# Delta-rule values and two gated branch outputs turned by VectorE in blocks of 32 and through DRAM, in place of TensorE transposes

## The chip, the cores and the metric

The kernel runs on one core of one Trainium2 chip, as one launch. The metric is the device time in microseconds (us). The kernel before takes 1671.04 us (median of 3 runs, 1670.95 to 1672.13).

A core has engines that each work through their own list of instructions in order: TensorE (PE in the profile; its weight loads are PEld), VectorE (DVE), ScalarE (ACT), GpSimd (POOL) and SyncE (SP). They wait for each other by semaphores. SP and POOL issue the DMA transfers here: SP streams the weights in, POOL issues everything small.

## The reference

One decoder layer over 256 positions of width 2048, all in float32: `x + mixer(rms_norm(x))`, then `x + ffn(rms_norm(x))`, then a last norm. Three branches of the mixer are projected out of one matrix product, and the change concerns two of them, the delta rule (GDN, 8 value heads of 128) and the gated linear attention (GLA, 4 heads of 256):

```
h = rms_norm(x);  c_q, ..., gla_q, gla_k, gla_v, ..., gdn_qkv, ..., gdn_z, merge = split(h @ w_in)
# GDN: conv + SiLU gives q, k, v; per chunk of 64 a triangular solve with v
u0  = triangular_solve(t_mat, beta * v)
o   = rms_norm(delta_rule(...)) ;  y_gdn = o * silu(z)
# GLA: chunked scan with a decay for each key channel
o   = rms_norm(gla_scan(...))   ;  y_gla = o * silu(r)
mixed = sum_i sigmoid(merge_i) * (y_i @ w_branch_i);  x + mixed @ w_out
```

## The kernel before, in words

**Weights.** Every weight goes the same way, in pieces of 512 KB: SP loads `raw`; ACT writes its rounded part `hi` (`split_piece`, act.copy, L191 in the profile); DVE writes the rest, `lo` = raw - hi (the subtraction stands under L103, the line of the helper `tt`); PE multiplies with both. The stream pool holds four buffers each of `raw`, `hi` and `lo`, so ACT and DVE can be some four pieces ahead of PE and no more. `t_chunk` (L237 to L239) computes 256 positions by 512 columns into two banks of PSUM; `fj_chunk` (L212, L213) computes 256 columns by 256 positions, also into two banks (here with half-pieces' products side by side, added up afterwards).

**PSUM.** There are two groups of four banks: `acc` for these weight products, `mix` (tiles `ps`) for all else. A fifth `acc` tile takes the bank of the first, as soon as that has been read. A chunk of `fj_chunk` is read by `halves_sum` (L217 to L221): for both of its banks ACT copies one half out, and DVE adds the other half.

**Delta rule (GDN).** Its convolution leaves the values `gv` with channels on the partitions. Before the solves, PE transposes them (L781, 16 transposes of 128x128 into four `ps` tiles), and DVE scales them from PSUM into `vt` (four instructions 128x512). Solves and state updates follow for heads in pairs `gp`; each pair leaves `og` tiles (`o_gdn`, DVE copies at L834), of which ACT takes squares (`junk`, L840). Once all four `og` are there, DVE computes their inverse norms (a chain of small instructions, `m`, `rsy`, `rsa`, `fg`), and `gated_out` multiplies each `og` by its gate `zs` and by `fg`, has PE transpose it (L865, 16 in all), and splits the result from PSUM into `hi_y` (ACT, L293) and `lo_y` (DVE, L106), the operand of the branch's projection.

**GLA.** Then the memory of the region `r2` (which held the delta rule's tiles, among them four rotating buffers of the tag `t`) is given up and `r3` opened, in the same memory. GLA's query and key products `lq` and `lk` are computed by `fj_chunk` (two chunks each), its values `lv` and its gate (`gates_of(GLA_R)`) by `t_chunk`. Head by head, DVE and ACT then compute exponentials (tiles `E`) for small matmuls on PE; behind each head's work stands a quarter of the merge of the delta rule's branch, whose projection reads `hi_y` and `lo_y`. At the end `gated_out` runs for GLA's outputs `ol` (16 more transposes), into `hi_E` and `lo_E`.

**The order of the work.** The program is written in the order of the formulas; a scheduler of the tile framework then moves instructions within each engine's list, by its own model of their durations. A pool's tile that is reused waits for all who read the earlier one, DMA transfers out of it among them.

**A turn.** `turned` exists before, and is used for the merged outputs and the residual stream: DVE transposes each 32x32 block of a tile within its place (a STREAM_TRANSPOSE, L304), POOL issues a DMA that writes the tile to DRAM (L306), and four DMAs read it back with the blocks exchanged (L312).

Of the kernel before, what the change touches and what calls it, by code (L numbers as in the profile page):

```python
# [16 lines left out]
P = 128  # L17
# [38 lines left out]
def trunk(ctx, tc, A, out, dbg=None, stop=None):  # L56
# [4 lines left out]
    def nm(s):  # L61
        serial[0] += 1
        return f"{s}{serial[0]}"
# [18 lines left out]
    def S(tag, shape=(P, 512), dt=F32, n=None):  # L82
        p, bufs = pools[tag]
        return p.tile(list(shape), dt, name=nm(n or tag), tag=tag, bufs=bufs)

    def PS(n="ps"):
        return pp.tile([P, 512], F32, name=nm(n), tag="mix")
# [7 lines left out]
    def keep(shape, n, dt=F32):  # L95
        return cp.tile(list(shape), dt, name=n)
# [5 lines left out]
    def tt(o, a, b, op, eng=None):  # L102
        (eng or dve).tensor_tensor(o, a, b, op=op)  # L103
# [138 lines left out]
    def TH():  # L242
        return wp.tile([P, 512], F32, name=nm("th"), tag="th", bufs=4)
# [51 lines left out]

    def turned(src, tags, n=512):

        nk = n // P  # L300
        d = dp.tile([2 * P, n], F32, name=nm("d_t"))
        for t in range(2):
            v = S(tags[0], (P, n), n="tr")
            dve.transpose(v.rearrange("p (b k i) -> p k b i", b=4, k=nk),  # L304
                          src[t].rearrange("p (k b i) -> p k b i", b=4, k=nk))
            pool.dma_start(d[t * P:(t + 1) * P], v)  # L306
        dv = d.rearrange("(a j) (b k i) -> b j a k i", j=32, b=4, k=nk)
        res = []
        for g in range(nk // 2):
            r = S(tags[1], (P, 8, 2, 32), n="rd")  # L310
            for b in range(4):
                pool.dma_start(r[b * 32:(b + 1) * 32], dv[b, :, :, 2 * g:2 * g + 2])  # L312
            res.append(r)
        return res

# [320 lines left out]


    sel = keep([P, 68], "sel", F32R)
    pool.memset(sel.bitcast(F32), 0.0)
# [134 lines left out]
    for gp in ((0, 1), (2, 3)):  # L774

        vts = {}
        for g in gp:
            psb = PS().rearrange("p (t x) -> p t x", t=2)
            for a in range(2):
                for t in range(2):  # L780
                    pe.transpose(psb[:, t, a * P:(a + 1) * P], gvv[2 * g + a][:, t * P:(t + 1) * P], ident)  # L781
            vts[g] = S("vt", (P, 2, 2, P))
            tt(vts[g].rearrange("p t a d -> p t (a d)"), psb, vs[:, :, g:g + 1].to_broadcast([P, 2, 256]), MUL)
        for s in (32, 64):
# [70 lines left out]

    def gated_out(o_tiles, f_of, zs, gcol, name, ytag):

        y = Act(8, ytag)
        for g in range(4):
            o = o_tiles[g]  # L860
            f_of(g, o, [zs[t][g // 2][:, (g % 2) * 256:(g % 2) * 256 + 256] for t in range(2)])
            psb = PS()
            for a in range(2):
                for t in range(2):
                    pe.transpose(psb[:, a * 256 + t * P:a * 256 + (t + 1) * P], o[:, t, a, :], ident)  # L865
            gained(psb, [half_gain[:, gcol + 2 * g + a:gcol + 2 * g + a + 1] for a in range(2)], y)
            if dbg is not None and ("y_" + name) in dbg:
                full = S("t", (P, 2, 256), n="dbg")
                tt(full, y.hi[g].bitcast(F32), y.lo[g], ADD)
                sync.dma_start(dbg["y_" + name][:, 2 * g:2 * g + 2, :], full)  # L870
        return y
# [53 lines left out]

    y_gdn = gated_out(o_gdn, scale_gdn, zs, 8, "gdn", "y")
    if stop == "gdn":
# [18 lines left out]

    sr = gates_of(GLA_R, "rs", "d")


# [119 lines left out]

    y_gla = gated_out(o_gla, scale_gla, sr, 0, "gla", "E")  # L1070
    if stop == "gla":
# [208 lines left out]
```

## Time and profile before

| | |
|---|---|
| time, median of 3 runs | 1671.04 us |
| profiled execution | 1671.5 us, its span 1669.7 us, granted clock 0.998 |
| PE busy | 1656.2 us, 99% of the span |
| DVE busy | 1106.4 us, 66% |
| ACT busy | 828.0 us, 50% |
| POOL busy | 135.7 us, 8% |
| chain that ended last | PE 94%, DVE 1% |
| moved by DMA | 314.96 MB, 188 GB/s to and from HBM over the span |

The span is what the profile covers; 1.8 us of the execution's own time lie around it. "Busy" leaves waits out, and matmuls overlap each other, so a busy PE need not be PE at its peak. Times within the span are counted from its start.

### The profile page before, as it was taken

How to read it: one execution, taken by the hardware profiler on the slowest of the kernel's cores; microseconds unless marked ns; L12 is line 12 of the kernel's file. 1: busy time of each engine (PE TensorE's matmuls, PEld its weight loads, DVE VectorE, ACT ScalarE, POOL GpSimd, SP SyncE). 2: the span in 40 equal slices, each digit the busy share in tenths (PEclk: the TensorE clock that was granted, in tenths of full speed). 3: DMA queues.
4: the chain of work that ended last, by engine and by line, in shares of the span. 5: the costliest groups of instructions: out<-in, count | busy, mean ns of one | idle time of the engine just before them, and what ended most of it. 6: DMA issues, size and time to landing. Idle time of an engine off the chain costs nothing.

```text
span 1669.7 us, 23887 instructions
## 1 busy us (share of the span) xinstructions
PE 1656.2 (99%) x9068; PEld 1406.8 (84%) x9068; DVE 1106.4 (66%) x1740; ACT 828.0 (50%) x1157; POOL 135.7 (8%) x202
## 2 busy tenths in 40 slices
PE   9999999999999999999999999999999999999997
PEld 7898888888888888888888888888888888888886
DVE  6868798755755795755656766664566665556666
ACT  6555563433444654444445654454355553345454
POOL 1000032200000000002112000000000000000000
PEclk9999999999999999999999999999999999999999
DMA  7565556654565456568777665656666566665653
GB/s 267 147 201 153 158 155 190 206 155 148 160 186 192 153 189 180 174 204 254 231 225 244 205 190 190 188 188 190 194 193 191 189 190 191 193 191 187 199 186 117
DMA packets 181059, 314.96 MB, mean 189 GB/s; under 512 B 17786, under 2 KB 45106, under 8 KB 180944
## 3 DMA queue, kind: packets, MB, share of 16 engines
q1 hardware_dynamic: 175488, 301.83, 57.7%
q0 software_dynamic: 5424, 11.60, 2.4%
q8 instruction: 71, 1.16, 0.3%
q14 instruction: 44, 0.36, 0.1%
q10 hardware_dynamic: 32, 0.01, 0.0%
HBM read 307.63 MB, written 5.77 MB: 188 GB/s over the span
## 4 chain that ended last, share of the span: by engine, by line
PE 94%; DVE 1%; issue 0%; ACT 0%; ACTq 0%
PE acc L239 17%; PE acc L237 17%; PE acc L238 17%; PE acc L212 15%; PE mix L212 10%; PE acc L213 8%; PE mix L213 5%; PE acc L1204 0%; PE acc L1206 0%; PE acc L1205 0%; PE ps L542 0%; PE ps L543 0%; DVE lo L103 0%; DVE u L103 0%; PE ps L1026 0%; PE ps L796 0%
## 5 line engine op out<-in xcount | busy, mean ns | idle before, releaser
L103 DVE TENSOR_TENSOR lo<-raw,hi 128x1024 fp32r<-128x1024 f32 (+2 forms) x571 | 686.6, 1205 | 498.9 <-ACT hi L191 496.1
L191 ACT CAST hi<-raw 128x1024 fp32r<-128x1024 f32 (+2 forms) x555 | 582.1, 1049 | 702.4 <-PE acc L239 412.2
L212 PE MATMUL acc<-hl_h,hi 128*128 128x512 f32 x1088 | 383.5, 397 | 0.0
L213 PE MATMUL acc<-hl_h,lo 128*128 128x256 f32 x1088 | 304.5, 280 | 0.0
L238 PE MATMUL acc<-lo,hl_h 128*128 128x512 f32 x640 | 249.3, 392 | 0.0
L239 PE MATMUL acc<-hi,hl_h 128*128 128x512 f32 x640 | 248.8, 392 | 0.0
L237 PE MATMUL acc<-hi,hl_h 128*128 128x512 f32 x640 | 247.4, 392 | 0.1
L212 PE MATMUL mix<-hl_h,hi 128*128 128x512 f32 x704 | 246.3, 395 | 0.0
L212 PEld LDWEIGHTS acc<-hl_h,hi 128*128 128x128 f32 x1088 | 203.9, 188 | 47.1
L213 PEld LDWEIGHTS acc<-hl_h,lo 128*128 128x128 f32 x1088 | 205.0, 188 | 1.0
L213 PE MATMUL mix<-hl_h,lo 128*128 128x256 f32 x704 | 196.0, 278 | 0.0
L212 PEld LDWEIGHTS mix<-hl_h,hi 128*128 128x128 f32 x704 | 132.1, 188 | 31.6
L237 PEld LDWEIGHTS acc<-hi,hl_h 128*128 128x128 f32 x640 | 120.3, 188 | 25.6 <-ACT hl_h L293 0.5
L238 PEld LDWEIGHTS acc<-lo,hl_h 128*128 128x128 f32 x640 | 120.5, 188 | 24.7
L239 PEld LDWEIGHTS acc<-hi,hl_h 128*128 128x128 f32 x640 | 120.3, 188 | 24.7
L213 PEld LDWEIGHTS mix<-hl_h,lo 128*128 128x128 f32 x704 | 132.5, 188 | 0.0
L238 PE MATMUL acc<-lo,hi_f 128*128 128x512 f32 x320 | 124.3, 389 | 0.0
L237 PE MATMUL acc<-hi,hi_f 128*128 128x512 f32 x320 | 124.2, 389 | 0.0
L239 PE MATMUL acc<-hi,lo_f 128*128 128x512 f32 x320 | 124.0, 389 | 0.0
L103 POOL TENSOR_TENSOR fcv<-fcv,rbc 128x512 f32<-128x512 f32 x22 | 31.3, 1424 | 669.0 <-ACT fcv L1161 669.0
L239 PEld LDWEIGHTS acc<-hi,lo_f 128*128 128x128 f32 x320 | 60.1, 188 | 12.5
L237 PEld LDWEIGHTS acc<-hi,hi_f 128*128 128x128 f32 x320 | 60.1, 188 | 12.5
(407 smaller groups left out, 1928.8 us busy)
## 6 DMA issues: line engine op xcount, KB each, us to landing
raw<-in_w_in_dram SPq DMA_DIRECT2D x207, 512.0 KB, 3.4
raw<-in_ffn_w_up_dram SPq DMA_DIRECT2D x176, 512.0 KB, 3.7
raw<-in_ffn_w_down_dram SPq DMA_DIRECT2D x88, 512.0 KB, 4.6
raw<-in_w_out_dram SPq DMA_DIRECT2D x32, 512.0 KB, 4.7
raw<-in_w_branch_mla_dram SPq DMA_DIRECT2D x16, 512.0 KB, 3.8
raw<-in_w_branch_gdn_dram SPq DMA_DIRECT2D x16, 512.0 KB, 3.8
raw<-in_w_branch_gla_dram SPq DMA_DIRECT2D x16, 512.0 KB, 6.1
raw<-in_mla_w_ukv_dram SPq DMA_DIRECT2D x8, 512.0 KB, 4.5
```

What stands on the lines that cost most here:

```text
L103: (eng or dve).tensor_tensor(o, a, b, op=op)
L191: act.copy(hi[:, ks], raw[:, ks])
L212: pe.matmul(banks[f], hi[:, kt, fs], joint[k], start=k == 0, stop=False, skip_group_check=True)
L213: pe.matmul(banks[f][:, :T], lo[:, kt, fs], joint[k][:, :T], start=False, stop=k == nk - 1, skip_group_check=True)
L237: pe.matmul(o, ah, hi[:, kt, :], start=first, stop=False)
L238: pe.matmul(o, ah, lo[:, kt, :], start=False, stop=False)
L239: pe.matmul(o, al, hi[:, kt, :], start=False, stop=last)
```

## The change

Three transposes by PE are replaced.

- The delta rule's values: right after the decay `gdec`, DVE turns the blocks of each `gv` tile (4 STREAM_TRANSPOSE of 128x512 into tiles of the tag `t`), and POOL writes them to DRAM (`d_v`, 4 DMAs). Before each pair's solves, POOL reads them back with blocks exchanged (16 DMAs, `rd`), and DVE scales them into `vt` (8 instructions 128x256 instead of 4 of 128x512).
- The delta rule's outputs: `gated_out` now scales each `og` as before, and turns it out: 8 STREAM_TRANSPOSE of 128x256 into tiles `tr` of the tag `t`, which has four buffers, and 8 DMAs to DRAM. `gated_in` reads it back (16 DMAs, into tiles `th` of the stream pool) and splits it from SBUF into `hi_y` and `lo_y`. It is called a stage later, behind `gates_of(GLA_R)`.
- GLA's outputs: the same two functions, one right after the other, with tiles of the tag `lqkv`.

No transposes of PE remain in these three places: 48 fewer. ACT and DVE have the same number of splits. DVE has 20 block transposes more, POOL 68 more DMAs to issue.

```diff
-    def turned(src, tags, n=512):
+    def turn_out(src, tag, n=512):
         nk = n // P
         d = dp.tile([2 * P, n], F32, name=nm("d_t"))
         for t in range(2):
-            v = S(tags[0], (P, n), n="tr")
+            v = S(tag, (P, n), n="tr")
             dve.transpose(v.rearrange("p (b k i) -> p k b i", b=4, k=nk),
                           src[t].rearrange("p (k b i) -> p k b i", b=4, k=nk))
             pool.dma_start(d[t * P:(t + 1) * P], v)
...
+        return d.rearrange("(a j) (b k i) -> b j a k i", j=32, b=4, k=nk)
+
+    def turn_in(dv, g, tag):
+        r = S(tag, (P, 8, 2, 32), n="rd") if tag else TH().rearrange("p (a k i) -> p a k i", k=2, i=32)
+        for b in range(4):
+            pool.dma_start(r[b * 32:(b + 1) * 32], dv[b, :, :, 2 * g:2 * g + 2])
+        return r
...
+    d_v = []
+    for g in range(4):
+        v = S("t", (P, 4, 4, 32), n="tr")
+        dve.transpose(v.rearrange("p b k i -> p k b i"), gv[g].rearrange("p a (t b i) -> p (a t) b i", t=2, b=4))
+        d = dp.tile([P, 4, 4, 32], F32, name=nm("d_v"))
+        pool.dma_start(d, v)
+        d_v.append(d.rearrange("(a j) b k i -> b j a k i", j=32))
...
         for g in gp:
-            psb = PS().rearrange("p (t x) -> p t x", t=2)
-            for a in range(2):
-                for t in range(2):
-                    pe.transpose(psb[:, t, a * P:(a + 1) * P], gvv[2 * g + a][:, t * P:(t + 1) * P], ident)
+            r = S("t", (P, 4, 2, 2, 32), n="rd")
+            for b in range(4):
+                pool.dma_start(r[b * 32:(b + 1) * 32].rearrange("p c a t i -> p c (a t) i"), d_v[g][b])
             vts[g] = S("vt", (P, 2, 2, P))
-            tt(vts[g].rearrange("p t a d -> p t (a d)"), psb, vs[:, :, g:g + 1].to_broadcast([P, 2, 256]), MUL)
+            for t in range(2):
+                dve.tensor_scalar(vts[g][:, t].rearrange("p a (c i) -> p a c i", i=32),
+                                  r[:, :, :, t].rearrange("p c a i -> p a c i"), vs[:, t, g:g + 1], None, op0=MUL)
...
-    def gated_out(o_tiles, f_of, zs, gcol, name, ytag):
-        y = Act(8, ytag)
+    def gated_out(o_tiles, f_of, zs, tag):
+        res = []
         for g in range(4):
             o = o_tiles[g]
             f_of(g, o, [zs[t][g // 2][:, (g % 2) * 256:(g % 2) * 256 + 256] for t in range(2)])
-            psb = PS()
-            for a in range(2):
-                for t in range(2):
-                    pe.transpose(psb[:, a * 256 + t * P:a * 256 + (t + 1) * P], o[:, t, a, :], ident)
-            gained(psb, [half_gain[:, gcol + 2 * g + a:gcol + 2 * g + a + 1] for a in range(2)], y)
...
+            res.append(turn_out([o[:, t].rearrange("p a d -> p (a d)") for t in range(2)], tag, 256))
+        return res
+
+    def gated_in(dvs, gcol, ytag, tag):
+        y = Act(8, ytag)
+        for g in range(4):
+            gained_sb(turn_in(dvs[g], 0, tag),
+                      [half_gain[:, gcol + 2 * g + a:gcol + 2 * g + a + 1] for a in range(2)], y)
         return y
...
-    y_gdn = gated_out(o_gdn, scale_gdn, zs, 8, "gdn", "y")
+    d_gdn = gated_out(o_gdn, scale_gdn, zs, "t")
...
     sr = gates_of(GLA_R, "rs", "d")
+    y_gdn = gated_in(d_gdn, 8, "y", None)
...
-    y_gla = gated_out(o_gla, scale_gla, sr, 0, "gla", "E")
+    y_gla = gated_in(gated_out(o_gla, scale_gla, sr, "lqkv"), 0, "E", "lqkv")
```

Where the scheduler puts these instructions is seen in each engine's list. The number behind a tile's name tells one buffer from another, and differs between the two programs; "waits" names the semaphores for which a row waits: those of an engine, or those of POOL's DMAs (DMASW0 to 7, handed out in turn) and SP's (DMAHW).

**DVE, from the last `og` tiles to GLA's first query sums.** `og` are the delta rule's outputs, `zs` the gates, `m` the first tile of the inverse norms, `lq` GLA's queries, `acc` banks of PSUM. Before, this stood there:

```order
L834 COPY og_3096<-ps_3089 128x512 [waits PE_49]
L834 COPY og_3113<-ps_3106 128x512 [waits PE_49]
L103 TENSOR_TENSOR og_3096<-og_3096,zs_4367 128x256 [waits DVE_49,Activation_49]
L103 TENSOR_TENSOR og_3096<-og_3096,zs_4371 128x256 [waits Activation_49]
L103 TENSOR_TENSOR og_3113<-og_3113,zs_4367 128x256 [waits DVE_49,Activation_49]
L103 TENSOR_TENSOR lo_4603<-raw_4600,hi_4602 128x1024 [waits DMAHW0_49,PE_49,Activation_49]
L103 TENSOR_TENSOR m_3127<-m_3127,gst 128x16 [waits Activation_49]
L103 TENSOR_TENSOR og_3113<-og_3113,zs_4371 128x256
L951 COPY glr_5433<-few 16x256
L103 TENSOR_TENSOR lq_4433<-lq_4433,acc_4437 128x256 [waits Activation_49]
L103 TENSOR_TENSOR lq_4433<-lq_4433,acc_4438 128x256 [waits Activation_49]
```

Now the first query sum stands behind the whole scaling and the eight block transposes (the rows shown begin at the last product with `fg`):

```order
L103 TENSOR_TENSOR og_3133<-og_3133,fg 128x512
L302 STREAM_TRANSPOSE tr_4397<-og_2948 128x2x4x32 [waits DVE_49]
L302 STREAM_TRANSPOSE tr_4400<-og_2948 128x2x4x32
L302 STREAM_TRANSPOSE tr_4407<-og_2965 128x2x4x32 [waits DVE_49]
L302 STREAM_TRANSPOSE tr_4410<-og_2965 128x2x4x32
L302 STREAM_TRANSPOSE tr_4417<-og_3116 128x2x4x32 [waits DMASW5_49,DVE_49]
L302 STREAM_TRANSPOSE tr_4420<-og_3116 128x2x4x32 [waits DMASW6_49,DVE_49]
L302 STREAM_TRANSPOSE tr_4427<-og_3133 128x2x4x32 [waits DMASW7_49,DVE_49]
L302 STREAM_TRANSPOSE tr_4430<-og_3133 128x2x4x32 [waits DMASW0_49,DVE_49]
L964 COPY glr_5481<-few 16x256
L103 TENSOR_TENSOR lq_4437<-lq_4437,acc_4441 128x256 [waits DMASW4_49,Activation_49]
L103 TENSOR_TENSOR lq_4437<-lq_4437,acc_4442 128x256 [waits Activation_49]
```

The four block transposes that name a DMASW wait for the write of the tile that had their buffer (DMASW5, 6, 7 and 0 are the first four of the eight writes, in order), and the first sum for the eighth write (DMASW4): the memory of `lq` in `r3` was that of `r2`'s last `tr`. Between the two copies of `og` and this sum stands one weight piece's `lo`; none stands between that `lo` and the sum. ACT's copy of the same bank, on which the sum waits as well, waits for the same write.

**PE, the first product for GLA's keys** (`acc_4627` before, `acc_4631` now, the fifth `acc` bank from the first of the query chunks on). Before, the last rows ahead of it are the second query chunk's:

```order
L213 MATMUL acc_4533<-hl_h_209,lo_4603 128x256
L212 MATMUL acc_4533<-hl_h_219,hi_4602 128x512
L213 MATMUL acc_4533<-hl_h_219,lo_4603 128x256
L212 MATMUL acc_4533<-hl_h_220,hi_4602 128x512
L213 MATMUL acc_4533<-hl_h_220,lo_4603 128x256
L212 MATMUL acc_4627<-hl_h_142,hi_4631 128x512 [waits DVE_49,Activation_49]
```

Now they are the delta rule's last outputs (`ps_3126`, which the second copy to `og` reads):

```order
L213 MATMUL acc_4537<-hl_h_220,lo_4607 128x256
L844 MATMUL ps_3126<-W_3107,hq_2661 128x128 [waits DVE_49]
L842 MATMUL ps_3126<-W_3089,hq_2660 128x128
L843 MATMUL ps_3126<-W_3089,hq_2660 128x128
L844 MATMUL ps_3126<-W_3107,hq_2661 128x128
L212 MATMUL acc_4631<-hl_h_142,hi_4635 128x512 [waits DVE_49]
```

The solves and outputs of the delta rule stand later among the weight pieces than before. The DVE instruction for which the last row waits is the first query sum shown above (`lq_4437` with `acc_4441`).

**PE, where the merge of the delta rule's branch begins**, among GLA's first head (`hl_h` are the layer's inputs, for the merge gate; `hi_y` the branch's). Before, the merge gate's seventh piece is begun like this:

```order
L237 MATMUL acc_5605<-hi_5717,hl_h_208 128x512 [waits Activation_49]
L237 MATMUL acc_5606<-hi_5717,hl_h_208 128x512
L238 MATMUL acc_5605<-lo_5718,hl_h_208 128x512 [waits DVE_49]
L239 MATMUL acc_5605<-hi_5717,hl_h_208 128x512
L237 MATMUL acc_5605<-hi_5717,hl_h_209 128x512
```

Now two products of the branch's own first piece are in between:

```order
L237 MATMUL acc_5653<-hi_5765,hl_h_208 128x512 [waits Activation_49]
L237 MATMUL acc_5654<-hi_5765,hl_h_208 128x512
L237 MATMUL acc_5803<-hi_5807,hi_y_5442 128x512 [waits Activation_49]
L237 MATMUL acc_5804<-hi_5807,hi_y_5442 128x512
L238 MATMUL acc_5653<-lo_5766,hl_h_208 128x512 [waits DVE_49]
```

The new third row waits for ACT's cast of the branch's first piece (`hi_5807`), two pieces further on; in ACT's list that cast stands behind three pairs of `hi_y` splits, which before stood ahead of GLA's key sums, and behind exponentials of the first head.

More of the change, by code (lines that the diff above doesn't have):

```diff
@@ L306, in turned @@
             pool.dma_start(d[t * P:(t + 1) * P], v)
[L307 to L314, printed above, removed]
+        return d.rearrange("(a j) (b k i) -> b j a k i", j=32, b=4, k=nk)
[4 more added lines that the diff above has]
+        return r
+    def turned(src, tags, n=512):
+        dv = turn_out(src, tags[0], n)
+        return [turn_in(dv, g, tags[1]) for g in range(n // 256)]
     def gained_sb(r, gains, store):
@@ L861, in gated_out @@
             f_of(g, o, [zs[t][g // 2][:, (g % 2) * 256:(g % 2) * 256 + 256] for t in range(2)])
-            psb = PS()
-            for a in range(2):
-                for t in range(2):
-                    pe.transpose(psb[:, a * 256 + t * P:a * 256 + (t + 1) * P], o[:, t, a, :], ident)
-            gained(psb, [half_gain[:, gcol + 2 * g + a:gcol + 2 * g + a + 1] for a in range(2)], y)
[L867 to L870, printed above, removed]
+            res.append(turn_out([o[:, t].rearrange("p a d -> p (a d)") for t in range(2)], tag, 256))
[5 more added lines that the diff above has]
+                      [half_gain[:, gcol + 2 * g + a:gcol + 2 * g + a + 1] for a in range(2)], y)
         return y
```

## The prediction

> **What bounds the kernel now.** I read the page's busy times and its chain first, then what PE waited for, then, around the places that the change touches, the timelines of PE, DVE, ACT and POOL.
>
> ```profile
> PE 1656.2 (99%) x9068; PEld 1406.8 (84%) x9068; DVE 1106.4 (66%) x1740; ACT 828.0 (50%) x1157; POOL 135.7 (8%) x202
> ...
> PE 94%; DVE 1%; issue 0%; ACT 0%; ACTq 0%
> ```
>
> ```profile
> PE acc L1204 <- ACT hi_f L266: 1.1, 1, 1.1
> PE warm L159 <- DVE ones L155: 1.1, 1, 1.1
> PE ps L364 <- DMA x<-in_x_dram: 0.9, 1, 0.9
> PE acc L198 <- DVE lo L103: 0.5, 2, 0.4
> ```
>
> PE is busy 99% of the span, 94% of the chain that ended last is PE's, and all its waits together are 3.6 us. So two things set the new time, and nothing else: what PE no longer does, and what PE must newly wait for. DVE's and ACT's busy shares, 66% and 50%, only say that they have room on average; where their instructions stand decides.
>
> **What PE no longer does.** 48 transposes go. The line view of L865 gives sixteen of them (duration in ns, first and last start):
>
> ```profile
> L865 PE MATMUL ps<-ident,og x16: 271/272/273, 454.4 to 456.0; 128*128 128x128 f32 x16
> ```
>
> Sixteen in a row start within 1.6 us, one each 0.107 us (the 272 ns are a matmul's pipeline, which overlaps the next). 48 of them are 5.1 us, with the last one's drain in each group 5.2. All lie on PE's path: 5.2 us less.
>
> **Where a new wait stands.** I take the moment at which PE issues the last products of the delta rule's output as zero. In the trace this is 434.63 us, where PE goes straight on with weights:
>
> ```profile
> 434.49 0.39 PE L832 MATMUL ps<-W,hq 128*128 128x128 f32 x2
> 434.63 0.48 PE L212 MATMUL acc<-hl_h,hi 128*128 128x512 f32 x1
> ```
>
> In the changed order the next PE instruction is the first key product. It needs the fifth `acc` bank, that is the first one again, and that is free only when DVE has added the first query sum; DVE's list has the whole scaling and all eight block transposes ahead of that sum. PE cannot run ahead of it: there is nothing else in its list. So PE stands still for as long as DVE takes from zero to that sum. Before, the same sums were done 5 us after the copies of `og` (the row at 439.85 below), and PE had a query chunk to work on meanwhile. DVE's rows of before give the lengths:
>
> ```profile
> 434.91 0.69 DVE L834 COPY og<-ps 128x512 f32<-128x512 f32 x1 [0.20 <-PE ps L832]
> ...
> 437.87 1.23 DVE L103 TENSOR_TENSOR lo<-raw,hi 128x1024 fp32r<-128x1024 f32 x1 [0.51 <-ACT hi L191]
> 439.01 0.17 DVE L103 TENSOR_TENSOR m<-m,gst 128x16 f32<-128x16 f32 x1
> ...
> 439.85 0.75 DVE L103 TENSOR_TENSOR lq<-lq,acc 128x256 f32<-128x256 f32 x2
> ...
> 443.74 0.17 DVE L103 TENSOR_TENSOR rsa<-rsy 128x16 f32<-128x16 f32 x1
> ...
> 444.56 0.17 DVE L103 TENSOR_TENSOR rsa<-rsa,rsm 128x16 f32<-128x16 f32 x1
> ...
> 449.71 2.49 DVE L103 TENSOR_TENSOR og<-og,fg 128x512 f32<-128x512 f32 x4
> ```
>
> From zero: the copy begins at 0.28 and takes 0.69 (1.0 us); one `lo`, 437.87 to the next start 439.01, 1.14 (2.1); four products with `zs`, of the size of the `lq` sums (0.75 for two), 0.35 each (3.5); the small ones: four at some 0.1, ten that depend on each other at 0.205 (four steps from 443.74 to 444.56), and 0.4 for the last pair (6.3); four products with `fg`, 2.4 (8.7).
>
> Then the turn. Before has the same operation on tiles twice as wide, two 256-KB writes with the reads that wait for them, and for 128 KB the inverses' writes:
>
> ```profile
> 860.92 1.30 DVE L304 STREAM_TRANSPOSE tr<-x 128x512 f32<-128x512 f32 x2
> ```
>
> ```profile
> 861.92 1.14 POOL L306 DMA_DIRECT2D d_t<-tr  x2 [16.09 <-DVE tr L304]
> 867.82 2.34 POOL L312 DMA_DIRECT2D rd<-d_t  x4 [4.76 <-issue]
> ```
>
> ```profile
> 319.12 1.07 POOL L759 DMA_DIRECT2D d_y<-xt  x2 [47.49 <-DVE xt L103]
> 322.70 2.20 POOL L768 DMA_DIRECT2D Y<-d_y  x4 [2.51 <-DMA d_y<-xt]
> ```
>
> A transpose of half the width is 0.35 us (an estimate: half of 0.65 and a little). The first ends at 9.05; its write is issued 0.35 later (861.92 against the first transpose's end, about 861.57), at 9.4; POOL issues one each 0.57, so the fourth write at 11.1. Transposes five to eight each wait for the write that empties their buffer. From issue to release a write takes 3.05 us by the 128-KB row (second issue 319.65 to 322.70) and 5.3 by the 256-KB one (862.49 to 867.82). Ours are 128 KB, so I take 3.3, near the first: four are in flight, and their rows are half as long. The eighth transpose ends at 11.1 + 3.3 + 0.35 = 14.75, its write is issued at 15.1 and releases at 18.4. Only now ACT copies the query bank's half, and DVE adds the other, 0.31 and 0.37 (two sums in 0.75; the copies' row is this):
>
> ```profile
> 438.05 0.62 ACT L220 COPY lq<-acc 128x256 f32<-128x256 f32 x2
> ```
>
> With 0.2 for the two wake-ups that is 19.3 us. By 3.05 twice it is 18.8, by 5.3 twice 23.3. This is the large term: PE waits 19.3 us (18.8 to 23.3), once. Behind it four weight pieces stand ready, and while PE works on them ACT and DVE make the next: no second wait there.
>
> **A second new wait.** Where GLA's first head and the merge of the delta rule's branch begin, DVE and ACT are already full, and three pairs of `hi_y` now stand ahead of a cast that PE needs.
>
> ```profile
> 564.73 1.28 ACT L971 ACT_TABLE_LOAD   x1
> 566.02 0.63 ACT L971 ACTIVATE ge<-ge 128x512 f32<-128x512 f32 x1
> 566.56 1.04 ACT L191 CAST hi<-raw 128x1024 fp32r<-128x1024 f32 x1
> ...
> 574.59 1.15 ACT L1006 ACTIVATE E<-E 128x512 f32<-128x512 f32 x2
> ```
>
> ```profile
> 455.01 2.81 ACT L293 ACTIVATE hi_y<-ps,half_gain 128x256 fp32r<-128x256 f32 x7 [1.15 <-PE ps L865]
> ```
>
> ```profile
> 577.01 0.61 PE L237 MATMUL acc<-hi,hl_h 128*128 128x512 f32 x2
> ```
>
> Behind the `ge` that ends at 566.65 ACT has, up to that cast's end, three pairs of `hi_y` (0.8 a pair: 2.4), four casts (4.2), three table loads (3.85), two more `ge` (1.2) and three `E` (1.7): 13.3 us, so 579.95. PE is there after the two products at 577.01, at 577.5. It waits about 2.5 us. The ends are 0 (if it overtakes) and 4.5 (if ACT also waits for the read-backs).
>
> **What costs nothing.** The delta rule's values: the first two read-backs stand ahead of POOL's write of the inverses and put it off by 8 issues of 0.58, 4.6 us. The solves stand later in PE's list and cover it; if not, they would wait for some of these 4.6 us. The eight new scalings come to as much DVE time as the four from PSUM that go. GLA's outputs: eight writes, then the first four reads, are there after 8 x 0.57 + 3.3 + 4 x 0.585 + 5.3 = 15.5 us; ahead of the first product with `hi_E` PE has a merge gate's eight pieces of twelve products, at 0.235 each (rows at 10.74 and 11.21 below) 22.5 us. Without that cover it would be those 15.5 us.
>
> **The restart.** After a standstill PE may be slow at first. The only start in this trace is the kernel's own:
>
> ```profile
> 8.26 1.22 PE L237 MATMUL acc<-hi,hl_h 128*128 128x512 f32 x2
> 9.28 1.06 PE L238 MATMUL acc<-lo,hl_h 128*128 128x512 f32 x2
> 10.14 0.77 PE L239 MATMUL acc<-hi,hl_h 128*128 128x512 f32 x2
> 10.74 0.63 PE L237 MATMUL acc<-hi,hl_h 128*128 128x512 f32 x2
> 11.21 0.63 PE L238 MATMUL acc<-lo,hl_h 128*128 128x512 f32 x2
> ```
>
> The first three pairs take 1.02, 0.86 and 0.60 us from start to start, the next 0.47: 1.1 us more. I add 1.1 (0 to 1.8). [...]
>
> **The sum.** 1671.5 - 5.2 + 19.3 + 2.5 + 1.1 = 1689.2 us for the profiled execution. That one lies 0.46 us above the median, so 1688.7.
>
> **Rivals.** (1) *The waits for writes do not bind*: the buffers were free or the writes land before they are asked for. Then the eight transposes run through (2.8 us), the sum is done at 8.7 + 2.8 + 0.7 = 12.2, and the time is 1671.0 - 5.2 + 12.2 + 2.5 + 1.1 = 1681.6. For it: the write of half the size has no row of its own. Against it: the order shows the waits, and the shorter of the two rows is 3.05 us. (2) *The second place is worse*: the read-backs come late on POOL, which has 16 to issue at 0.58 us, while ACT holds the casts behind them; a missed group of four costs up to 2.3 us there, and with the upper ends of the large term it gives 1693 to 1697. For it: DVE and ACT are full there. Against it: buffers for the first two groups are free early. (3) *Faster*: the bank is not what holds PE. If ACT and DVE read the query bank before the scaling, as before, or PE had other work until then, PE would not stop and only the removed transposes would count: 1671.0 - 5.2 = 1665.8. It decides at one point: whether the first query sum ends before PE's last delta-rule product. Against it: DVE's list is in order, and the sum stands some 19 us behind that product. [...]
>
> **How the numbers follow.** The forecast, one long wait with the writes in it, has 0.72; rival 1 has 0.13, rival 2 has 0.10, the faster one 0.05. The range goes from 1680 us, which takes in rival 1, to 1696, which takes in the upper end of the write and most of rival 2; about 0.1 to 0.15 is left out. What a measurement of this kernel can tell from no change is 0.2%, 3.3 us. Slower by more than that: 0.93; faster: 0.05; within: 0.02.
>
> **What would show it.** PE's waits should list one of about 19 us (first product of a key chunk, released by DVE's `lq` sum), and in PE's slices or windows a hole near 430 to 450 us. DVE should show transposes five to eight with idle time that ends with a DMA `d_t<-tr`; ACT's `lq` copy should end an idle stretch with the same. Near 570 to 580 us PE should wait some 2 us for ACT's cast. PE's busy time should fall by about 5 us. I am wrong if PE has no wait of over 10 us, or if the long one is released by something else.

## The result, and the profile after

The changed kernel takes 1690.36 us (median of 4 runs, 1689.78 to 1691.13). The kernel before, on the same chip, takes 1671.14 us (4 runs, 1670.95 to 1672.13). The ratio is 1.0116, with a 95% interval of 1.0104 to 1.0128: slower by 19.2 us. The profiled execution took 1690.41 us, with a span of 1688.6.

The page of the changed kernel: PE's busy time fell by 1.0 us only; products at half clock (granted 0.50, below) count as busy for longer, which is some 3 us. PE's share of the chain went from 94% to 90%. One slice of 42 us, the eleventh (422 to 464 us), holds a hole, and the row of PE's granted clock (`PEclk`, 9 is full) shows it too.

```profile
PE 1655.2 (98%) x9020; PEld 1404.4 (83%) x9020; DVE 1114.7 (66%) x1764; ACT 827.4 (49%) x1157; POOL 175.5 (10%) x270
...
PE   9999999999699999999999999999999999999997
...
PEclk9999999999899999999999999999999999999999
...
PE 90%; issue 3%; DVE 1%; ACT 1%; POOL 0%; DMA 0%; ACTq 0%; POOLq 0%
```

PE's waits in the changed kernel (us in total, times, longest). These two are new; the others are none above 1.1 us, as before.

```profile
PE acc L212 <- DVE lq L103: 16.6, 1, 16.6
PE acc L237 <- ACT hi L191: 2.9, 1, 2.9
```

The long one, in the timelines of the changed kernel (start, duration, instruction, idle time before it and what ended it). PE first: behind the delta rule's last products there is nothing, then the first key product.

```profile
445.65 0.39 PE L844 MATMUL ps<-W,hq 128*128 128x128 f32 x2
462.65 0.80 PE L212 MATMUL acc<-hl_h,hi 128*128 128x512 f32 x1 [16.61 <-DVE lq L103]
```

DVE, POOL and ACT in the same stretch:

```profile
452.13 2.49 DVE L103 TENSOR_TENSOR og<-og,fg 128x512 f32<-128x512 f32 x4
454.55 1.41 DVE L302 STREAM_TRANSPOSE tr<-og 128x256 f32<-128x256 f32 x4
457.36 2.04 DVE L302 STREAM_TRANSPOSE tr<-og 128x256 f32<-128x256 f32 x4 [1.40 <-DMA d_t<-tr]
...
462.17 1.41 DVE L103 TENSOR_TENSOR lq<-lq,acc 128x256 f32<-128x256 f32 x4 [2.35 <-ACT lq L220]
```

```profile
455.28 2.18 POOL L304 DMA_DIRECT2D d_t<-tr  x4 [42.76 <-DVE tr L302]
458.10 2.14 POOL L304 DMA_DIRECT2D d_t<-tr  x4 [0.65 <-DVE tr L302]
```

```profile
461.77 1.20 ACT L220 COPY lq<-acc 128x256 f32<-128x256 f32 x4 [13.31 <-DMA d_t<-tr]
```

Scaling, four transposes, a wait for the first write (455.28 to 457.36, 2.1 us), four more transposes, a wait of ACT for the last write (issued about 459.7, released at 461.77, 2.1 us again), copy, sum: the chain of the prediction, link by link. PE stands from about 445.8 to 462.65, 16.9 us by its starts.

The short one, PE in the timeline of the changed kernel, at the first product with the delta rule's branch:

```profile
592.32 0.61 PE L237 MATMUL acc<-hi,hl_h 128*128 128x512 f32 x2
595.83 1.22 PE L237 MATMUL acc<-hi,hi_y 128*128 128x512 f32 x2 [2.89 <-ACT hi L191]
596.84 0.63 PE L238 MATMUL acc<-lo,hl_h 128*128 128x512 f32 x1
597.27 0.63 PE L239 MATMUL acc<-hi,hl_h 128*128 128x512 f32 x1
```

PE waits 2.9 us (3.05 by starts) for ACT's cast, and then its products start 0.43 us apart instead of 0.23, until 598.95: the granted clock is half there (0.50 from 596 to 598 us, 0.55 from 598 to 599).

### The profile page after: what moved, and what is told of

Same layout as the page of the kernel before. It is cut to its first block, busy times and chain, and to the rows that moved or that the text cites. A ratio compares the mean times of both kernels' runs of the same rounds, so it can differ in the third digit from the quotient of the medians.

```text
span 1688.6 us, 23965 instructions
## 1 busy us (share of the span) xinstructions
PE 1655.2 (98%) x9020; PEld 1404.4 (83%) x9020; DVE 1114.7 (66%) x1764; ACT 827.4 (49%) x1157; POOL 175.5 (10%) x270
## 4 chain that ended last, share of the span: by engine, by line
PE 90%; issue 3%; DVE 1%; ACT 1%; POOL 0%; DMA 0%; ACTq 0%; POOLq 0%
PE acc L239 16%; PE acc L237 16%; PE acc L238 16%; PE acc L212 14%; PE mix L212 10%; PE acc L213 7%; PE mix L213 5%; PE acc L1217 0%; PE acc L1219 0%; PE acc L1218 0%; PE ps L544 0%; PE ps L545 0%; DVE lo L103 0%; PE ps L1039 0%; DVE u L103 0%
## 5 line engine op out<-in xcount | busy, mean ns | idle before, releaser
L212 PE MATMUL acc<-hl_h,hi 128*128 128x512 f32 x1088 | 385.3, 399 | 16.6 <-DVE lq L103 16.6
L238 PEld LDWEIGHTS acc<-lo,hi_f 128*128 128x128 f32 x320 | 60.1, 188 | 12.5
L239 PEld LDWEIGHTS acc<-hi,lo_f 128*128 128x128 f32 x320 | 60.1, 188 | 12.5
```

The source lines that it names most:

```text
L212: pe.matmul(banks[f], hi[:, kt, fs], joint[k], start=k == 0, stop=False, skip_group_check=True)
L238: pe.matmul(o, ah, lo[:, kt, :], start=False, stop=False)
L239: pe.matmul(o, al, hi[:, kt, :], start=False, stop=last)
```

## The experiments

The theory that went in: PE stands still twice, both times because of the turn of the delta-rule outputs; the turns of the values and of the GLA outputs cost nothing. The main rivals: some of the loss belongs to those two, or the writes do not bind. Each run is compared with the kernel before in the same series (1670.5 to 1670.9 us); the intervals are at 95%.

### 1. The delta-rule outputs back on PE (e1_gdn_on_pe)

The delta-rule outputs are transposed by PE again; values and GLA outputs stay turned. `gated_out_pe` is the `gated_out` of the kernel before.

```diff
-    d_gdn = gated_out(o_gdn, scale_gdn, zs, "t")
+    y_gdn = gated_out_pe(o_gdn, scale_gdn, zs, 8, "y")
...
-    y_gdn = gated_in(d_gdn, 8, "y", None)
```

> The gated outputs of the delta rule are transposed by PE again; the delta-rule values and the GLA outputs stay with VectorE. Theory (both stops of PE belong to the turn of the delta-rule outputs, and the other two turns cost nothing): no wait of PE above 2 us is left, 32 transposes by 0.107 us are still gone, so 1671.1 - 3.4 = 1667.7 us. Rival (some of the loss comes from the other two turns, the 1.3 us that the two stops and their restarts do not explain): 1669 us or more, with a new wait or a slower stretch near the delta-rule solves or after the GLA outputs.

Measured: 1673.93 us, ratio 1.0017 (1.0008 to 1.0026). The theory said 1667.7, so it falls: the other two turns cost some 6 us. The place was not where the rival looked for it. It is the old one, in the timeline of PE:

```profile
445.12 0.39 PE L844 MATMUL ps<-W,hq 128*128 128x128 f32 x2
449.60 0.50 PE L212 MATMUL acc<-hl_h,hi 128*128 128x512 f32 x1 [4.09 <-DVE lq L103]
```

The query sum now stands ahead of the scaling, as before, and still PE waits 4.1 us for it. The delta rule's last products are issued at 445.1, against 434.5 before the change, and the key products follow at once; in the kernel before, PE went on with query products at that point. So what the values' turn takes away is the work behind the delta rule. DVE's timeline, before the change:

```profile
209.31 0.69 DVE L103 TENSOR_TENSOR sq<-gq 128x512 f32<-128x512 f32 x1
```

and in this run:

```profile
208.73 1.30 DVE L643 STREAM_TRANSPOSE tr<-gv 128x512 f32<-128x512 f32 x2
...
226.56 0.70 DVE L643 STREAM_TRANSPOSE tr<-gv 128x512 f32<-128x512 f32 x1
227.19 0.65 DVE L103 TENSOR_TENSOR sq<-gq 128x512 f32<-128x512 f32 x1
```

The squares of q and k, from which the delta rule's norms come, start 18 us late, right behind the transposition of the last value tile. Later POOL adds to it, in this run's timeline:

```profile
333.00 4.36 POOL L791 DMA_DIRECT2D rd<-d_v  x8 [47.40 <-DVE el L103]
337.39 1.11 POOL L770 DMA_DIRECT2D d_y<-xt  x2
343.31 2.20 POOL L779 DMA_DIRECT2D Y<-d_y  x4 [4.80 <-DMA d_y<-xt]
```

The inverses are read back at 343.3, against 322.7 before. New theory: the values' turn makes the delta rule late, through the squares above all, and PE's list, which is fixed, then has its query products ahead of the delta rule's end instead of behind it.

### 2. The delta-rule outputs alone (e2_gdn_alone)

The edit undoes the other two: values and GLA outputs go through PE as in the kernel before.

```diff
-    y_gla = gated_in(gated_out(o_gla, scale_gla, sr, "lqkv"), 0, "E", "lqkv")
+    y_gla = gated_out_pe(o_gla, scale_gla, sr, 0, "E")
...
-            r = S("t", (P, 4, 2, 2, 32), n="rd")
...
+                    pe.transpose(psb[:, t, a * P:(a + 1) * P], gvv[2 * g + a][:, t * P:(t + 1) * P], ident)
```

> Only the gated outputs of the delta rule are turned through DRAM; the delta-rule values and the GLA outputs are transposed by PE as before. Theory: both stops of PE stay as they were (16.6 and 2.9 us in the list of waits) and 32 transposes by 0.107 us come back: 1690.4 + 3.4 = 1693.8 us. Rival (the other two turns carry the unexplained 1.3 us): 1692.5 us.

Measured: 1687.52 us, ratio 1.0098 (1.0084 to 1.0112): below both forecasts. PE's timeline:

```profile
446.17 0.28 PE L213 MATMUL acc<-hl_h,lo 128*128 128x256 f32 x1
456.76 0.77 PE L212 MATMUL acc<-hl_h,hi 128*128 128x512 f32 x1 [10.31 <-DVE lq L103]
```

Without the values' turn PE has query products until 446.2, 12.3 us after it had left the delta rule (433.85), and the long wait is 10.3 us instead of 16.6. The short one stays at 2.9. This bears out the new theory from the other side: the long stop belongs to two of the three turns.

### 3. Own buffers for the turned outputs (e3_own_buffers)

The changed kernel, with the eight turned tiles in a group of eight buffers that is free by then and whose memory the query sums do not take over.

```diff
-    d_gdn = gated_out(o_gdn, scale_gdn, zs, "t")
+    d_gdn = gated_out(o_gdn, scale_gdn, zs, "hq")
```

> The eight turned tiles of the delta-rule outputs get eight buffers of their own instead of four, in memory that the query sums do not take over; the order of the instructions is the same. Theory (the two waits for writes are part of the long stop): transposes five to eight run straight on, so the eight end at 454.55 + 4 x 0.35 = 456.0 us on the trace's clock instead of 458.8 or later, the query sum follows at 456.4, and PE's long wait falls from 16.6 to 10.5 us; the rest of it, scaling and transposes, stays: about 1684.3 us. Rival 1 (the writes do not bind, DVE's order alone makes the stop): 1690.4 us. Rival 2 (without the order nothing would be left to wait for): under 1675 us.

Measured: 1685.97 us, ratio 1.0090 (1.0076 to 1.0103). DVE's timeline:

```profile
455.76 2.72 DVE L302 STREAM_TRANSPOSE tr<-og 128x256 f32<-128x256 f32 x8
...
458.83 1.42 DVE L103 TENSOR_TENSOR lq<-lq,acc 128x256 f32<-128x256 f32 x4
```

Eight transposes without a gap, the sum behind them, and PE's wait is 12.1 us instead of 16.6. The writes cost 4.5 us of it, and rival 1 of this run (they do not bind) is out. The forecast of 10.5 us had counted only four of the eight transposes, 1.4 us too little.

### 4. The sums ahead of scaling and turn (e4_sums_first)

The changed kernel, with `gated_out` moved behind the query and key sums.

```diff
-    d_gdn = gated_out(o_gdn, scale_gdn, zs, "t")
...
             stt(out_[i], out_[i], f, rb1, MUL, MUL)
+    d_gdn = gated_out(o_gdn, scale_gdn, zs, "t")
     lv = [[None, None], [None, None]]
```

> The scaling and turn of the delta-rule outputs stand behind the query and key sums in the program, so that DVE adds the first query sum ahead of them; the four buffers and their waits for writes stay. Theory (the bank held by the query sum behind the turn is the whole long stop): PE's wait of 16.6 us and its slow restart of 1.5 us are gone, the short stop stays: 1690.4 - 16.9 - 1.5 = 1672.0 us. Rival (DVE's 12 us of scaling, turn and waits hold PE wherever they stand): a wait of PE of 5 us or more at a value chunk's bank or at a weight's lo part, 1677 us or more.

Measured: 1678.58 us, ratio 1.0041 (1.0029 to 1.0054). The number is the rival's, the reason is not. PE's waits list the same 4.1 us for the query sum as run 1, with DVE's sum now ahead of the scaling with `fg` and of the turn, and the 2.9 us for the cast:

```profile
PE acc L212 <- DVE lq L103: 4.1, 1, 4.1
```

The eight transposes and their writes hold nobody behind the sums. So 12.5 of the 16.6 us go with the order of scaling, turn and sum, and the 4.1 that stay are the ones that run 1 had without any turn of these outputs.

### 5. The GLA outputs alone (e5_gla_alone)

Both delta-rule edits are undone, the values as in run 2 and the outputs as in run 1; GLA's line stays as changed.

```diff
-    d_gdn = gated_out(o_gdn, scale_gdn, zs, "t")
+    y_gdn = gated_out_pe(o_gdn, scale_gdn, zs, 8, "y")
...
-            r = S("t", (P, 4, 2, 2, 32), n="rd")
...
+                    pe.transpose(psb[:, t, a * P:(a + 1) * P], gvv[2 * g + a][:, t * P:(t + 1) * P], ident)
```

> Only the GLA outputs are turned through DRAM; the delta-rule values and outputs are transposed by PE as before. Theory now (the values' turn carries all of the cost that showed with the delta-rule outputs back on PE, the GLA turn is free): no new wait, 16 transposes by 0.107 us gone, 1671.0 - 1.7 = 1669.3 us. Rival (the GLA turn costs it, for example its read-backs are late for the branch's first products): 1672 us or more.

Measured: 1669.77 us, ratio 0.9994 (0.9985 to 1.0003). PE has no new wait; the theory's 1669.3 is inside the interval, and the rival's 1672 is not. The GLA turn costs nothing that shows, and the 16 transposes that it saves are too few to measure.

### 6. The values' turn behind the squares (e6_values_later)

Run 1 with one block moved: the four transposes and writes of the values stand behind the loop over the squares.

```diff
-    d_v = []
-    for g in range(4):
-        v = S("t", (P, 4, 4, 32), n="tr")
...
     for i, tl in enumerate(gq + gk):
...
+    d_v = []
+    for g in range(4):
+        v = S("t", (P, 4, 4, 32), n="tr")
...
     srow = S("t", (4, 512), n="srow")
```

> Delta-rule outputs on PE as in the first run, GLA outputs turned; the values are still turned through DRAM, but their four block transposes and writes stand behind the squares of q and k in the program, so that the squares no longer wait for buffers that the last value tile holds. Theory (the values' turn makes the delta rule late through those buffers, and so PE has used up its query products when the delta rule ends): 58 products of the query chunk, some 10 us, stand behind the last delta-rule product again, PE's wait of 4.1 us for the query sum and its restart go: 1673.9 - 4.3 - 1.2 = 1668.4 us. Rival (it is the eight read-backs ahead of the write of the inverses on POOL that make it late): the wait of about 4 us stays, 1673 to 1674 us.

Measured: 1666.52 us, ratio 0.9974 (0.9964 to 0.9984). PE's wait for the sum is gone from the list, and 7.4 us with it. DVE and POOL in this run:

```profile
208.36 0.68 DVE L103 TENSOR_TENSOR sq<-gq 128x512 f32<-128x512 f32 x1
```

```profile
317.90 4.37 POOL L789 DMA_DIRECT2D rd<-d_v  x8 [46.36 <-DVE xt L103]
322.26 1.12 POOL L768 DMA_DIRECT2D d_y<-xt  x2
328.40 2.21 POOL L777 DMA_DIRECT2D Y<-d_y  x4 [5.02 <-DMA d_y<-xt]
```

The squares are back at 208 us. The eight read-backs still stand ahead of the inverses' write and still put the inverses off, by 5.7 us against before (328.4 against 322.7); no wait of PE comes of those 5.7 us. So of the two delays that the values bring, the one at the squares decides.

### 7. The read-backs earlier (e7_early_reads)

The changed kernel, with the read-backs of the delta-rule outputs ahead of GLA's gate chunks.

```diff
+    y_gdn = gated_in(d_gdn, 8, "y", None)
     sr = gates_of(GLA_R, "rs", "d")
-    y_gdn = gated_in(d_gdn, 8, "y", None)
```

> The changed kernel with one edit: the read-backs and gains of the delta-rule outputs stand ahead of GLA's gate chunks in the program instead of behind them. Theory (the short stop is ACT's three pairs of scalings ahead of a cast in the full stretch): the wait of 2.9 us and its slow restart of 1.3 us go, the long stop stays: 1690.4 - 3.05 - 1.3 = 1686.0 us. Rival (ACT stands for read-backs that have not landed, and PE waits for a cast behind them in the query and key chunks): another wait of 2 us or more after the long stop, 1689 us or more.

Measured: 1690.84 us, ratio 1.0121 (1.0107 to 1.0135). The rival's number, with the wait at another place than it said: the short stop is gone, and the long one has grown by 5.9 us. ACT's timeline:

```profile
462.67 0.91 ACT L325 ACTIVATE hi_y<-th,half_gain 128x256 fp32r<-128x256 f32 x2 [14.32 <-DMA th<-d_t]
466.06 0.91 ACT L325 ACTIVATE hi_y<-th,half_gain 128x256 fp32r<-128x256 f32 x2 [2.48 <-DMA th<-d_t]
466.88 1.17 ACT L220 COPY lq<-acc 128x256 f32<-128x256 f32 x4
```

Two pairs of scalings, each of them waiting for a read-back, now stand on ACT ahead of the copy that the query sum needs. The scalings have left the place where ACT is full, and stand in the way at the other.

### 8. All three moves (e8_all_three)

The changed kernel with the moves of runs 6, 4 and 7 together.

```diff
-    d_v = []
...
     for i, tl in enumerate(gq + gk):
...
+    d_v = []
...
-    d_gdn = gated_out(o_gdn, scale_gdn, zs, "t")
...
             stt(out_[i], out_[i], f, rb1, MUL, MUL)
+    d_gdn = gated_out(o_gdn, scale_gdn, zs, "t")
...
+    y_gdn = gated_in(d_gdn, 8, "y", None)
     sr = gates_of(GLA_R, "rs", "d")
-    y_gdn = gated_in(d_gdn, 8, "y", None)
```

> All three turns through DRAM as in the change, with three moves in the program: the values' transposes behind the squares, scaling and turn of the delta-rule outputs behind the query and key sums, their read-backs ahead of GLA's gate chunks. Theory (all that was lost are three places in the order, and nothing that the turns need by themselves): no wait of PE above 1.2 us, 48 transposes by 0.107 us gone: 1671.0 - 5.2 = 1665.8 us, faster than both kernels. Rival (DVE and ACT have too much to do in this stretch, whatever the order): waits of 3 us or more somewhere between the delta rule and GLA's first head, 1669 us or more.

Measured: 1664.49 us, ratio 0.9964 (0.9952 to 0.9977): faster than both kernels, by 6.4 us than before and by 25.9 us than the change. All three turns still go through DRAM. The page and PE's waits of this run:

```profile
PE 1650.5 (99%) x9020; PEld 1400.9 (84%) x9020; DVE 1113.3 (67%) x1764; ACT 828.4 (50%) x1157; POOL 176.7 (11%) x270
```

```profile
PE acc L1213 <- ACT hi_f L266: 1.1, 1, 1.1
PE warm L159 <- DVE ones L155: 1.1, 1, 1.1
PE ps L366 <- DMA x<-in_x_dram: 0.6, 2, 0.4
```

The longest wait is 1.1 us, and both of that length were there before. With the sums out of the way the early read-backs, which lengthened the long wait by 5.9 us in run 7, hold nobody. DVE does the same 1764 instructions as in the changed kernel and is as busy; only their order differs. The rival (too much to do, whatever the order) is out.

### 9. The values' move alone (e9_values_later_alone)

The changed kernel with the move of run 6.

```diff
-    d_v = []
...
     for i, tl in enumerate(gq + gk):
...
+    d_v = []
```

> The changed kernel with one edit: the values' block transposes and writes stand behind the squares of q and k. Scaling, turn and read-backs of the delta-rule outputs stay as changed. Theory (the values' turn is the part of the long stop that took PE's query products away): 58 products, 10.1 us, stand behind the last delta-rule product again; in return DVE has three more weight parts by 1.15 us ahead of the query sum. The long wait falls from 16.6 to 16.6 - 10.1 + 3.4 = 9.9 us, near the 10.3 us of the run without the values' turn: 1690.4 - 6.7 = 1683.7 us. Rival 1 (the stop is DVE's stretch alone and does not ask what PE has to do): 1690 us. Rival 2 (the query products count in full, DVE's further work lies beside its waits for writes): 6.5 us, 1680.3 us.

Measured: 1686.28 us, ratio 1.0091 (1.0076 to 1.0107). PE's long wait is 13.2 us: less than the 16.6 of the change, so the stop does depend on the work that PE has left, but 3.3 us more than forecast. DVE's timeline:

```profile
450.89 0.45 DVE L302 STREAM_TRANSPOSE tr<-og 128x256 f32<-128x256 f32 x1 [0.17 <-DMA d_t<-tr]
453.98 0.77 DVE L302 STREAM_TRANSPOSE tr<-og 128x256 f32<-128x256 f32 x2 [2.65 <-DMA d_t<-tr]
...
457.71 1.41 DVE L103 TENSOR_TENSOR lq<-lq,acc 128x256 f32<-128x256 f32 x4 [2.64 <-ACT lq L220]
```

Here transposes seven and eight wait 2.65 us for a write, longer than in the changed kernel. Run 12 asks whether that is the difference.

### 10. The late read-backs alone (e10_late_reads)

Run 8 with the read-backs put back behind GLA's gate chunks.

```diff
-    y_gdn = gated_in(d_gdn, 8, "y", None)
     sr = gates_of(GLA_R, "rs", "d")
+    y_gdn = gated_in(d_gdn, 8, "y", None)
```

> The kernel with all three moves, with the read-backs and gains of the delta-rule outputs put back behind GLA's gate chunks, as in the change: only the short stop comes back. Theory (a stop of 3 us costs its length and a slow restart behind it): one wait of 2.9 us for ACT's cast and 1.3 us of slower products behind it, 1664.5 + 3.05 + 1.3 = 1668.9 us. Rival (the restart costs nothing by itself, PE makes it up): 1667.5 us or less. Rival 2 (the short stop came only with the long one): no wait of over 1.2 us, 1664.5 us.

Measured: 1670.15 us, ratio 0.9999 (0.9990 to 1.0008), 5.7 us more than run 8. PE's waits list 2.9 us for the cast and no other new one. So the short stop comes without the long one, and it costs nearly twice its length. Why is seen in the windows of this run (us, busy time of PE, PEld, DVE, ACT and POOL, granted clock, DMA share, GB/s):

```profile
574.00:576.00 2.00, 0.00 (x0) 0.00 (x0) 2.00 (x7) 2.00 (x5) 0.00 (x0) 0.91 0.66 172
576.00:578.00 2.00, 1.51 (x4) 1.22 (x5) 2.00 (x7) 2.00 (x4) 0.00 (x0) 0.50 0.70 189
578.00:580.00 2.00, 2.00 (x6) 1.59 (x5) 2.00 (x9) 0.71 (x2) 0.00 (x0) 0.50 0.44 163
580.00:582.00 2.00, 2.00 (x6) 1.54 (x5) 2.00 (x6) 0.00 (x0) 0.00 (x0) 0.50 0.00 0
582.00:584.00 2.00, 2.00 (x23) 1.19 (x22) 2.00 (x3) 1.05 (x1) 0.00 (x0) 0.88 0.33 37
```

PE is at it again from 576.5, and the clock is half until about 582.5 (0.88 in the last row is 0.48 us at half): 6.0 us of products that start 0.43 instead of 0.23 us apart, 3.0 us lost. In the changed kernel the slow stretch behind the same stop was 3.1 us and cost 1.5. The rival without a restart is out. What it costs differs from run to run: the 11 runs lie between 1668.4 and 1673.4 us, and the profiled one, 1672.4, is one of the long ones.

### 11. Own buffers for the values (e11_values_own)

Run 1 again, with the values' turn at its old place and only its buffers changed: they come from the group `g` of eight, which the squares do not use.

```diff
-        v = S("t", (P, 4, 4, 32), n="tr")
+        v = S("g", (P, 4, 4, 32), n="tr")
```

> The first run's kernel (delta-rule outputs on PE, values and GLA outputs turned) with one edit: the four turned value tiles get four buffers of their own, at the same place in the program; the squares of q and k keep the four buffers they had. Theory (the squares are late because their buffers hold value tiles that wait for the last values and for their writes): the squares run from about 209 us as before the change, 38 query products, 6.6 us, stand behind the last delta-rule product, and the wait of 4.1 us goes: 1673.9 - 4.3 - 1.6 = 1668 us, within 2 us of the run with the values behind the squares. Rival (not the buffers, but the values' place ahead of the squares in the program makes them late): squares at 227 us and the wait of 4 us again, 1673 to 1674 us.

Measured: 1668.36 us, ratio 0.9986 (0.9977 to 0.9996). PE has no wait for the sum, and DVE's first square starts at 211.12 us instead of 227.19:

```profile
211.12 0.68 DVE L103 TENSOR_TENSOR sq<-gq 128x512 f32<-128x512 f32 x1
```

It is the buffers: in run 1 four were shared by four value tiles, the last of which exists only at about 226 us there, and by the squares behind them.

### 12. Values later and own buffers (e12_later_own)

Run 9 with the buffers of run 3.

```diff
-    d_gdn = gated_out(o_gdn, scale_gdn, zs, "t")
+    d_gdn = gated_out(o_gdn, scale_gdn, zs, "hq")
```

> The run with the values' turn behind the squares and everything else as changed, with one more edit: eight own buffers for the turned delta-rule outputs. Theory (the 13.2 us that PE waited there, 3.3 more than forecast, are writes that landed late): the eight transposes run on, with one weight part between, and end near 451.4 us, the query sum near 451.8, and PE waits 452.2 - 445 = 7.2 us: 1686.3 - 6 = 1680.3 us. What is left is the scaling and the transposes themselves. Rival (the 3.3 us are DVE's further weight parts): 10 to 11 us of wait, 1683.5 to 1684 us.

Measured: 1679.85 us, ratio 1.0055 (1.0041 to 1.0068). PE's timeline:

```profile
444.16 0.27 PE L213 MATMUL acc<-hl_h,lo 128*128 128x256 f32 x1
451.66 0.77 PE L212 MATMUL acc<-hl_h,hi 128*128 128x512 f32 x1 [7.22 <-DVE lq L103]
```

7.2 us, as the theory had it. With run 3 the long wait comes apart into three: 4.5 us for the writes (16.6 to 12.1), 4.9 for the products that the values' turn used up (12.1 to 7.2), 7.2 for the scaling and the transposes that stand ahead of the sum. Taken in the other order, run 9 first, it is 3.4 for the products and 6.0 for the writes: how these two share their 9.4 us depends on the order, the 7.2 does not.

## Why the prediction was right, and where not

The time was inside the range and 1.7 us from the point forecast, by the forecast's own case. That it came so near is in part luck: the long wait was sized 2.4 us too high, and terms that were too low or left out came to somewhat more. The steps:

- **What PE no longer does, 5.2 us.** Right in kind, a little low: without new waits the same removal gives 6.4 us (run 8). The sign "PE's busy time should fall by about 5 us" failed all the same: it fell by 1.0, and products that last longer at half clock are some 3 us of the difference.
- **The long wait, 19.3 us.** Right in chain, releaser and place in PE's list; 16.9 by PE's starts, and some 11 us later than the 434.6 from which it was counted, because the delta rule itself ended later (last item). The term that was mis-sized is the write, taken at 3.3 us from issue to release and twice in the chain: it was 2.1 both times, which is the whole 2.4 us. The nearer of the two rows of before, the inverses' write with 3.05 us, was nearer still than the value I took. The 0.2 us for the two wake-ups was my estimate; in the changed kernel the two gaps come to 0.1 us (ACT's first copy ends at 462.14, the sum runs from 462.17 to 462.59, PE starts at 462.65). In run 9, on the same tiles, one write took 4.0 us: it is a size that varies, and not a constant. The upper end, 5.3 us, was misread: the idle time of its row ends with "issue" and not with the write, which landed after 4.7 us in that trace.
- **Rival 1, the writes do not bind.** Out: without them the wait is 12.1 us (run 3).
- **Rivals 2 and 3.** The second place was not worse (2.9 us). The faster case was not this kernel's, since the sum does stand behind the scaling; run 8 makes it so that the sum does not, and its 1664.5 us lie near the 1665.8 of that rival.
- **The second wait, 2.5 us.** 3.05 by starts, and the releaser is the one named. Run 10 shows it alone.
- **The restart, 1.1 us.** Too low: 1.5 us behind each of the two stops (some 3.1 us of products at half clock each), where I had counted one restart. The 1.5 is not a constant either: run 10 lost 3.0 behind the same short stop. The rows from which I took the 1.1, at the kernel's start, have a granted clock of 1.00 (8 to 11 us, before), so they do not show the half clock (0.50) that the stops brought.
- **What costs nothing.** For the GLA outputs this held (run 5). For the delta rule's values it was wrong, and it is the step that failed: "The solves stand later in PE's list and cover it". I looked at the read-backs on POOL, which indeed cost nothing (run 6). I did not follow the other half of the edit, the four transposes and writes, to the squares that share their buffers: 18 us of delay at 209 us. The cover that I named was the very thing that was spent. PE did not stop for the late solves, it did its query products ahead of them, and then had none left when the delta rule ended.

That the sum came out all the same is because "there is nothing else in its list" was read from the changed order, where the loss was already in; only the cause was put in the wrong place. From "costs nothing" one would have said that undoing the delta-rule outputs' turn gives 1667.7 us, and it gave 1673.9 (run 1). Moved behind the squares by itself, the values' turn is worth 4.1 us in the changed kernel (run 9).

The profiled sum with the measured terms is 1671.5 - 6.0 + 16.9 + 1.5 + 3.05 + 1.5 = 1688.45, with 6.0 from the spans of before (1669.7) and run 8 (1663.7). The profiled execution took 1690.41. Of the 2.0 us that are left, some 1.2 arise ahead of 490 us and 0.8 between 590 and 650, when PE's products are counted off against those of run 8; what they are stays open.

## What to carry to other kernels

Work that is taken off the busiest engine is only won if nothing that this engine waits for stands behind the new work on another engine's list: the same turns gave 1.0116 in one order and 0.9964 in another. Of a step that is moved, follow each buffer group it draws from to the next user of that group, and ask from when the last tile of the step can exist. A delay that is hidden is paid for with the work that hides it; look at what that work was keeping busy before.

## What the hardware showed that I had not expected

The clock behind a longer standstill was not always the slower one. Behind the 2.9-us wait of the changed kernel and of run 10 the granted clock was already at half (0.50 from 596 to 598 us, and in run 10 from 576 to 578). Behind the 4.1-us wait of run 1 PE worked at its full pace for 1.2 us more, one pair of products every 0.35 us, and then at one every 0.64; PE's timeline there (the last products ahead of the fall, the first slow one, and the last):

```profile
450.40 0.40 PE L212 MATMUL acc<-hl_h,hi 128*128 128x512 f32 x1
450.64 0.32 PE L213 MATMUL acc<-hl_h,lo 128*128 128x256 f32 x1
450.76 0.62 PE L212 MATMUL acc<-hl_h,hi 128*128 128x512 f32 x1
...
453.96 0.49 PE L212 MATMUL acc<-hl_h,hi 128*128 128x512 f32 x1
```

PE was slow for 3.1 us behind both stops of the changed kernel (462.65 to 465.79 and 595.83 to 598.91), for 3.4 in run 1 (450.76 to about 454.2) and for 6.0 in run 10 (576.49 to 582.48). The stretches at half clock, the standstill included, were 17.1 us around the long stop of the changed kernel (448.7 to 465.8), 3.4 around its short one (595.5 to 598.9) and 6.8 in run 10 (575.6 to 582.5). The clock fell 2.7, 2.6 and 2.0 us after PE's last product had ended, at about 446.0, 592.9 and 573.6: the granted clock is 0.86 from 448 to 449 and 0.75 from 595 to 596 us in the changed kernel, and 0.91 from 574 to 576 in run 10. What decides when it falls and when it is full again no run shows. What a stop costs need not be the same in each execution either: of run 10's, the shortest (1668.4 us) had a mean granted clock of 0.998, the longest (1673.4) one of 0.996.

A write of 128 KB through DRAM released its buffer 2.1 us after its issue in the changed kernel, twice, and so did the first of run 9 (448.19 to 450.27). The third of run 9, on the same tiles, was issued at 449.98 and released its buffer only at 453.98, 4.0 us later. In the changed kernel nothing was moved from 452 us until these writes (DMA share 0.00 from 452 to 456), and up to 460 us they were alone. What made the one write of run 9 longer no run shows.
